# Retention ahead of the memory keys, the values inside the memory attention, and no lo parts on GpSimd

## The chip, the cores and the metric

The kernel runs on one core of a Trainium2 chip. The metric is the device time of one execution in microseconds. TensorE multiplies, ScalarE and VectorE do the element-wise work, GpSimd does a little of it, SyncE issues the loads. Weights stream from HBM into SBUF while the work goes on.

## The reference

Two blocks on 256 tokens of width 1024, in float32. The first block, cut to what matters here:

```python
x = x + parallel_mixer(rms_norm(x, norm_mix_w), w_in, ..., ret_gn_w, w_out)
x = x + memory_cross_attention(rms_norm(x, norm_mem_w), rms_norm(mem, norm_memkv_w),
                               w_mq, w_mkv, mem_q_norm_w, mem_k_norm_w, w_mo)
x = x + hierarchical_moe(rms_norm(x, norm_moe_w), w_group, w_router, ...)   # 32 experts, top 2
...
# parallel mixer: dilated attention beside retention in both directions
return jnp.concatenate([attn, ret], axis=-1) @ w_out
...
# memory attention
q = rms_norm(split_heads(h @ w_mq, MEM_HEADS, MEM_HEAD_DIM), q_norm_w) * (MEM_HEAD_DIM ** -0.5)
mk, mv = jnp.split(mem_h @ w_mkv, 2, axis=-1)
k = rms_norm(split_heads(mk, MEM_HEADS, MEM_HEAD_DIM), k_norm_w)
v = split_heads(mv, MEM_HEADS, MEM_HEAD_DIM)
```

The memory keys and values depend on `mem` alone, so they may be computed anywhere ahead of the memory attention. The second block has two layers, each a gated feed-forward, four token mixers, another feed-forward, with layer norms behind each.

## The kernel before

The 256 tokens are two token tiles of 128 partitions. Dense weights come in chunks of 1 MB (`raw`, a ring of four slots), in the order in which they are packed. To keep float32 accuracy each chunk, in two parts, is split exactly: `wh`, a rounded copy (ScalarE, L279), and `wl`, the rest (L283, a subtraction on VectorE or GpSimd). The tokens are split alike (`xh`, `xl`; ScalarE L391, VectorE L392). Every product is then three matmuls (`mm3`, L310 to L312). `s.pool_mod` and `s.on_pool` say which subtractions go to GpSimd: every fourth part, and some named ones.

Block 1 runs so: `mixer1` loads x, norms it with the gain `norm_mix_w` (a load that puts the 4 KB row on all 128 partitions), transposes it (L401) and projects; then dilated attention, the projections of retention, `mem_kv` (norm of the memory tokens, keys, values), `retention` and the out projection. `retention` has for each token tile two groups of heads: scores, a decay mask (`dtmp`, `dec`, `rsc`), value products (L718), then a norm per head (`normed`: statistics L679, L680, scaling L685, a power on GpSimd L418, scaling on ScalarE L690 and VectorE L692), and transposes of the result `rn`. `memory` norms, projects the queries (`mqn`, `mq`), then scores against the keys `mk`, softmax, values, out projection.

Meanwhile 21 chunks of the experts' weights are loaded into slots that come free (`moe_early`, `moe_slots`); the other 171 follow as the experts' products release slots. Ahead of the experts, `moe_start` computes the routes, and a branch (L889) goes into a long body only if an expert has more tokens than slots, which is not the case with these inputs.

All engines' instructions are put in order by a scheduler that simulates the program; the code's order decides which work exists at a time, and which slots of SBUF and PSUM it waits for. Transposes, retention's sums and the memory tokens' transposes share two PSUM banks (tag `tr`).

Of the kernel before, what the change touches and what calls it, by code (L numbers as in the profile page):

```python
# [26 lines left out]
# slots that the dense pools leave free, and those that memory()'s do  # L27
M_EARLY, M_MID = 6, 5

# projections (capitals; H: the heads of B) and attentions of the four mixers in the order of their issue  # L30
MIXERS = "BCHaDdAmw"
OUT = [k for k in MIXERS if k in "adwm"]
# the first gate and up tiles with tokens on partitions; the last down pairs with token tile 0 first, the norm of
# that tile after PLACE of the other's products
NAT, TAIL, PLACE = 2, 3, 4
# products of zeros that bring the tensor engine to its full clock while the first loads arrive
WARM = 18

# ------------------------------------------------------------------ host layout

def _nat(w):
    """[K, N] -> chunks [128, 4 k-tiles, <=512 columns], column groups outermost."""
    k, n = w.shape
    out = []
    for c in range(0, n, 512):
        g = w[:, c:c + 512].reshape(k // 128, 128, -1).transpose(1, 0, 2)
        for i in range(0, k // 128, 4):
            out.append(g[:, i:i + 4])
    return out


def _sq(w, halves=(0, 1)):
    """[1024, 1024] -> chunks [128, 4 k-tiles, 512 columns], halves of k outermost."""
# [4 lines left out]
def _trans(w):  # L58
    """[1024, N] -> chunks [128, 2 column tiles, 8 k-tiles, 128 columns]."""
# [19 lines left out]
def _pack_dense(i):  # L79
# [9 lines left out]
    ch += _nat(np.asarray(i["w_mkv"])[0])  # L89
    ch += _sq(np.asarray(i["w_out"])[0])  # L90
    ch += _nat(np.asarray(i["w_mq"])[0])
    ch += _sq(np.asarray(i["w_mo"])[0])
# [22 lines left out]
def _ffn_order():  # L115
    """Gate/up tiles and down pairs in the order of their use."""
# [55 lines left out]
def _pack_moe(i):  # L172
    """Per group of 4 experts: gate and up [k-tile][128, 4, 512], down [half][ff tile][128, 4, 512]."""
# [23 lines left out]
# ------------------------------------------------------------------ program  # L197

class Net:
    def __init__(s, ctx, tc, a, out):  # L200
        s.tc, s.nc, s.a, s.out = tc, tc.nc, a, out
        s.pos = 0
        s.on_pool = [None, None]
        s.pows, s.ahead = [], []
        s.dense_tags = ["a", "b"]
        s.nw, s.pool_mod = 0, 4
# [11 lines left out]
    # ---- storage  # L218
# [3 lines left out]
    def turn(s, tags):  # L222
        """The tags of a list in turn."""
# [3 lines left out]
    def banks(s):  # L227
        """Four accumulators, [token tile][half]."""
# [5 lines left out]
    def bcast(s, pool, name, n, off=0, tag=None, bufs=None, after=None):  # L234
        """A DRAM vector on every partition."""
# [7 lines left out]
    def column(s, pool, name, n, off=0, rep=1):  # L243
        """A DRAM vector down the partitions, rep times."""
# [7 lines left out]
    # ---- weights  # L252
# [12 lines left out]
    def weight(s, width=CH, parts=2, pool=None, own=None, cuts=1):  # L265
        """The next chunk, in parts, each as exact hi + lo, in the ring's tiles, pool's or own."""
# [3 lines left out]
        for i in range(parts):  # L270
# [13 lines left out]
            if eng is s.nc.gpsimd:  # L284
                s.pool_lo = i
# [5 lines left out]
    def own(s, p, i):  # L291
        """Tiles of pool p for a chunk."""
        return [[p.tile([128, CH // 2], F32R, name="own", tag=f"own{j}{k}{i}") for k in range(2)] for j in range(2)]

    def issue_after(s, i, j):
        """i, of the same engine as j, is issued after j."""
# [3 lines left out]
    def plan(s, spec):  # L300
        """Which of the next weight parts get their lo on GpSimd (not d), and after which of the last two powers."""
# [5 lines left out]
    # ---- products  # L307
# [6 lines left out]
    def dense_nat(s, x, n, done, stagger=False):  # L314
        """x @ W for n <= 512 columns, tokens on partitions; done(t, psum). stagger: token tile 0 first."""
# [25 lines left out]
    def dense_sq(s, x, done, halves=(0, 1), own=None, ahead=None):  # L341
        """x @ W for a square W, the k-tiles in halves, token tile 0 finished first; done(t, column half, psum).
        own: tiles for the parts of the last chunk."""
# [25 lines left out]
    def dense_trans(s, x, n, done):  # L369
        """(x @ W)^T for n <= 2 column tiles; done(i, psum[128, 256])."""  # L370
# [10 lines left out]
    # ---- operands  # L381
# [5 lines left out]
    def split(s, h, l, src, scale=None):  # L387
        """h + l = src * scale, exactly; scale a number or a column."""
# [8 lines left out]
    def transpose4(s, src, n=4, tag="tr"):  # L397
        """n blocks of 128 columns, transposed, in one bank."""
# [5 lines left out]
    def tsplit(s, x, t, src, k0=0, n=8, tag="tr"):  # L404
        """Token tile t of natural src (n k-tiles) into x[:, k0:]."""
# [7 lines left out]
    def rsqrt(s, v, n, scale, eps):  # L413
        """(v * scale + eps) ** -0.5; eps a number or a column."""
# [761 lines left out]
    def ln_state(s, p, x, li):  # L1176
# [3 lines left out]
        for t in range(NT):  # L1180
            xa.append(p.tile([128, D], F32, name=f"xa{t}"))
            i = s.nc.gpsimd.tensor_scalar(xa[t], x[t], ALPHA, None, op0=OP.mult)
            if li == 0:
                s.issue_after(i, s.pool_lo)
# [416 lines left out]
```

## Time and profile before

| | |
|---|---|
| time, median of 3 runs | 1754.07 us (1753.56 to 1755.35) |
| profiled execution, its span | 1753.4 us |
| TensorE busy | 1579.9 us, 90% |
| VectorE, ScalarE, GpSimd busy | 839.4, 657.0, 286.9 us |
| chain that ended last | TensorE 55%, loads 23%, VectorE 3% |
| TensorE's first expert gather | 284.73 us |

The profile gives no other time of the profiled execution than its span. The chain that ended last is followed back from the last instruction to whatever released it. Idle time of an engine counts only where that engine is waited for.

### The profile page before, as it was taken

Reading aid. Unit: us, or ns where it says so; the run is one execution under the profiler, and the core shown is the slowest. Engines: PE = TensorE matmul, PEld = TensorE weight load, DVE = VectorE, ACT = ScalarE, POOL = GpSimd, SP = SyncE. Lnnn points to the kernel's source line nnn. Section 1 sums busy time; section 2 is a strip of 40 time slices with the busy share of each in tenths; the row PEclk is TensorE's granted clock in tenths of the full one; section 3 lists DMA queues with packets and bytes.
Section 4 is the critical chain, followed back from the end, with each engine's and each line's share of the span. In section 5 each row is a group of like instructions: output and inputs, shape, how many; then the busy total and the mean of one; then the engine's idle time right before and its main releaser. Section 6 shows DMA issues by size and latency. Waiting matters only on the chain.

```text
span 1753.4 us, 24984 instructions
## 1 busy us (share of the span) xinstructions
PE 1579.9 (90%) x10070; PEld 1216.1 (69%) x10070; DVE 839.4 (48%) x1471; ACT 657.0 (37%) x1124; POOL 286.9 (16%) x253
## 2 busy tenths in 40 slices
PE   8999897877667767899999989999999999989998
PEld 6777784322211211599998769999999988779997
DVE  5657653100000000454477675556655667765555
ACT  4655441100000000344435745445444536734442
POOL 4223321100000000222224250000100032340000
PEclk9999998987878877999999989999999999989999
DMA  7444858999999999955554234556355634155552
GB/s 273 142 177 157 327 213 327 419 421 420 421 420 419 421 421 420 368 183 181 190 188 144 97 145 168 192 187 246 143 181 183 240 127 135 49 189 183 181 191 73
DMA packets 66186, 419.06 MB, mean 239 GB/s; under 512 B 10640, under 2 KB 12176, under 8 KB 18704
## 3 DMA queue, kind: packets, MB, share of 16 engines
q1 hardware_dynamic: 66064, 417.39, 62.8%
q8 instruction: 82, 1.34, 0.3%
q14 instruction: 40, 0.33, 0.1%
HBM read 416.32 MB, written 1.05 MB: 238 GB/s over the span
## 4 chain that ended last, share of the span: by engine, by line
PE 55%; DMA 23%; DVE 3%; POOL 1%; issue 1%; ACT 1%; DVEq 0%; SPq 0%; ACTq 0%; POOLq 0%
DMA mraw<-in_wm 23%; PE ps L310 17%; PE ps L312 17%; PE ps L311 17%; PE ps L401 1%; PE ps L480 1%; PE ps L950 1%; DVE xa L1169 1%; PE ps L970 0%; POOL rq L418 0%; PE ps L927 0%; DVE xl L392 0%; DVE lnst L1197 0%; DVE wl L283 0%; POOL ropet L1381 0%
## 5 line engine op out<-in xcount | busy, mean ns | idle before, releaser
L283 DVE TENSOR_TENSOR wl<-raw,wh 128x1024 fp32r<-128x1024 f32 (+2 forms) x314 | 389.3, 1250 | 302.0 <-ACT wh L279 301.1
L279 ACT ACTIVATE wh<-raw 128x1024 fp32r<-128x1024 f32 (+2 forms) x356 | 371.0, 1052 | 351.5 <-PE ps L311 181.1
L310 PE MATMUL ps<-xh,wh 128*128 128x256 f32 x1424 | 402.1, 282 | 3.4 <-ACT cv L1469 3.4
L312 PE MATMUL ps<-xh,wl 128*128 128x256 f32 x1424 | 401.4, 282 | 0.0
L311 PE MATMUL ps<-xl,wh 128*128 128x256 f32 x1424 | 401.0, 282 | 0.0
L310 PEld LDWEIGHTS ps<-xh,wh 128*128 128x128 f32 x1424 | 268.3, 188 | 6.6 <-ACT cv L1469 3.8
L311 PEld LDWEIGHTS ps<-xl,wh 128*128 128x128 f32 x1424 | 268.4, 189 | 1.4
L312 PEld LDWEIGHTS ps<-xh,wl 128*128 128x128 f32 x1424 | 268.4, 188 | 0.8
L950 PE MATMUL ps<-mraw,xg 128*32 128x512 f32 x1024 | 167.7, 758 | 77.4 <-DMA mraw<-in_wm 77.3
L312 PE MATMUL ps<-wh,xl 128*128 128x512 f32 (+3 forms) x520 | 190.1, 370 | 6.5 <-DVE xl L392 6.3
L310 PE MATMUL ps<-wh,xh 128*128 128x512 f32 (+3 forms) x520 | 190.5, 376 | 4.9 <-ACT xh L391 4.1
L311 PE MATMUL ps<-wl,xh 128*128 128x512 f32 (+3 forms) x520 | 191.9, 370 | 2.7 <-POOL wl L283 1.3
L950 PEld LDWEIGHTS ps<-mraw,xg 128*32 128x32 f32 x1024 | 25.6, 119 | 209.0 <-DMA mraw<-in_wm 173.0
L418 POOL TENSOR_TENSOR rq<-rv,mhalf 128x1 f32<-128x1 f32 (+4 forms) x46 | 46.9, 1020 | 728.1 <-DVE rv L416 720.4
L283 POOL TENSOR_TENSOR wl<-raw,wh 128x1024 fp32r<-128x1024 f32 x42 | 103.7, 2473 | 280.9 <-ACT wh L279 263.6
L956 DVE TENSOR_TENSOR mf<-ps,mf 128x512 f32<-128x512 f32 x8 | 5.5, 691 | 248.0 <-PE ps L950 244.1
L312 PEld LDWEIGHTS ps<-wh,xl 128*128 128x128 f32 x520 | 100.6, 194 | 23.2 <-DVE xl L392 10.4
L310 PEld LDWEIGHTS ps<-wh,xh 128*128 128x128 f32 x520 | 100.7, 195 | 22.7 <-ACT xh L391 7.6
L311 PEld LDWEIGHTS ps<-wl,xh 128*128 128x128 f32 x520 | 101.4, 195 | 18.4 <-POOL wl L283 3.4
L311 PE MATMUL ps<-wl,hf 128*128 128x512 f32 x256 | 100.1, 391 | 0.0
L312 PE MATMUL ps<-wh,hf 128*128 128x512 f32 x256 | 100.1, 391 | 0.0
L310 PE MATMUL ps<-wh,hf 128*128 128x512 f32 x256 | 98.2, 390 | 0.0
(357 smaller groups left out, 1981.0 us busy)
## 6 DMA issues: line engine op xcount, KB each, us to landing
mraw<-in_wm SPq DMA_DIRECT2D x191, 1024.0 KB, 19.9
raw<-in_wd SPq DMA_DIRECT2D x179, 1024.0 KB, 4.8
raw<-in_wd SPq DMA_DIRECT2D x8, 512.0 KB, 8.4
raw<-in_wd SPq DMA_DIRECT2D x4, 832.0 KB, 4.7
bc_ln_g<-in_ln_g SPq DMA_DIRECT2D x6, 512.0 KB, 5.7
bc_ln_b<-in_ln_b SPq DMA_DIRECT2D x6, 512.0 KB, 6.5
raw<-in_wd SPq DMA_DIRECT2D x4, 768.0 KB, 4.3
bias<-in_bias SPq DMA_DIRECT2D x4, 512.0 KB, 5.9
```

What stands on the lines that cost most here:

```text
L279: s.nc.scalar.activation(h[:, :n], rc, AF.Copy)
L283: i = eng.tensor_tensor(l[:, :n], rc, h[:, :n].bitcast(F32), op=OP.subtract)
L310: mm(out, lhsT=lh, rhs=rh, start=start, stop=False)
L311: mm(out, lhsT=lh, rhs=rl, start=False, stop=False)
L312: mm(out, lhsT=ll, rhs=rh, start=False, stop=stop)
L401: s.nc.tensor.transpose(ps[:, b * 128:b * 128 + 128], src[:, b * 128:b * 128 + 128], s.ident)
L418: s.last_pow = s.nc.gpsimd.tensor_tensor(q, r, s.mhalf[:, :n], op=OP.pow)
L480: s.nc.tensor.matmul(out, lhsT=v(j), rhs=pt[:, 2 * i + j], start=first and j == 0, stop=last and j == 1)
L950: nc.tensor.matmul(ps[32 * e:32 * e + 32], lhsT=xg[:, k, 32 * e:32 * e + 32], rhs=w[:, e * FF:e * FF + FF], start=k == 0, stop=k == NK - 1 ...
L956: nc.vector.tensor_tensor(f, gu[1], f, op=OP.mult)
L1169: nc.vector.scalar_tensor_tensor(z[:, cs], z[:, cs], mv[:, 0:1], g[:, cs], op0=OP.subtract, op1=OP.mult)
```

## The change

1. Order in block 1. `mem_kv` becomes `mem_k` (norm of the memory tokens and keys), called after `retention`, and `mem_v` (values), called in `memory` between the query projection and the scores. The weights are packed in the new order of use. The pools of the memory tokens lie on the other side of SBUF, and the out projection's extra tile has a pool of its own.
2. Start. The gain comes as a 4 KB row; a product with a column of ones puts it on all partitions, and VectorE copies it out of PSUM. The first raw chunk, in two halves, is issued ahead of token tile 1 of x. `moe_consts` (router weights and a triangle matrix) runs first.
3. No lo parts on GpSimd: `pool_mod` is 0 and no part is named, so 21 of block 1 and some 15 of the first feed-forward go to VectorE; eight in a later stage stay. One ordering rule that named the last such part is dropped.
4. The branch gets `preferred_fallthrough_block=False`: the short false path, a jump, stands behind the comparison, the body behind it.

Comments and docstrings go too, so line numbers differ.

```diff
-    ch += _nat(np.asarray(i["w_mkv"])[0])
+    mkv = np.asarray(i["w_mkv"])[0]
+    ch += _nat(mkv[:, :D])
     ch += _sq(np.asarray(i["w_out"])[0])
     ch += _nat(np.asarray(i["w_mq"])[0])
+    ch += _nat(mkv[:, D:])
...
-        s.on_pool = [None, None]
+        s.on_pool = []
...
-        s.nw, s.pool_mod = 0, 4
+        s.nw, s.pool_mod = 0, 0
...
-    def residual_out(s, x, o, ahead=None):
-        """x += o @ W for a square W; the operands before o are done with."""
-        w = s.xsp.tile([128, NK, S], F32R, name="xw", tag="xh").rearrange("p k n -> p (k n)")
+    def residual_out(s, x, o, ahead=None, pool=None):
+
+        w = (pool or s.xsp).tile([128, NK, S], F32R, name="xw", tag="xh").rearrange("p k n -> p (k n)")
...
     def mixer1(s):
+        s.moe_consts()
         x = [s.xp.tile([128, D], F32, name="x", tag=f"x{t}") for t in range(NT)]
...
+            one = p.tile([1, 128], F32, name="one")
+            s.nc.vector.memset(one, 1.0)
+            row = p.tile([1, D], F32, name="row")
+            s.nc.sync.dma_start(row, s.a["norm_mix_w"])
             for c in range(2):
                 cs = slice(c * 512, c * 512 + 512)
                 s.nc.sync.dma_start(x[0][:, cs], s.a["x"][:128, cs])
             s.nc.sync.dma_start(s.ident, s.a["ident"])
+            s.ahead = [s.raw(cuts=2)]
             s.nc.sync.dma_start(x[1], s.a["x"][128:])
-            wn = s.bcast(p, "norm_mix_w", D)
-            s.ahead = [s.raw(cuts=2)]
+            wn = p.tile([128, D], F32, name="wn")
+            for c in range(2):
+                cs = slice(c * 512, c * 512 + 512)
+                ps = s.bank("b")
+                s.nc.tensor.matmul(ps, lhsT=one, rhs=row[:, cs], start=True, stop=True)
+                s.nc.vector.tensor_copy(wn[:, cs], ps)
...
-            s.mem_kv()
-            s.on_pool = [None, False] * 3
             s.retention(r, o)
-        s.residual_out(x, o)
+            s.mem_k()
+        with ExitStack() as ctx:
+            s.residual_out(x, o, pool=s.pool(ctx, "xw1", side="right"))
         return x
...
-        ms = s.rms_operand(load, "norm_memkv_w")
+        s.ms = s.rms_operand(load, "norm_memkv_w", side="right")
         with ExitStack() as ctx:
-            p = s.pool(ctx, "memk")
+            p = s.pool(ctx, "memk", side="right")
             for c in range(2):
-                s.dense_nat(ms, 512, lambda t, ps: s.mem_normed(p, s.mk, c, t, ps, None))
+                s.dense_nat(s.ms, 512, lambda t, ps: s.mem_normed(p, s.mk, c, t, ps, None))
+
+    def mem_v(s):
+
         for c in range(2):
             def done(t, ps):
                 cs = slice(c * 512, c * 512 + 512)
-                nc.scalar.activation(s.mv[:, t, cs], ps, AF.Copy)
-            s.dense_nat(ms, 512, done)
+                s.nc.scalar.activation(s.mv[:, t, cs], ps, AF.Copy)
+            s.dense_nat(s.ms, 512, done)
...
-        s.moe_consts()
-        o = s.xsplit()
...
             s.moe_early(c0)
+            s.mem_v()
+            o = s.xsplit()
+            s.moe_slots(s.xsp, ["xl"])
...
-        with s.tc.If(cnt > CAP):
+        with s.tc.If(cnt > CAP, preferred_fallthrough_block=False):
             s.overflow(ht, x, r, hT, acc, late)
```

The first place is the start on VectorE. Before, the gain tile `bc_norm_mix_w` is a load, and the scales of x (`rms`) come first; `xl` is the lo part of the transposed tokens, `wl` a lo part of a weight chunk.

```order
L986 TENSOR_SCALAR ssb_156<-ss_155 128x1
L416 TENSOR_SCALAR rv_160<-ss_155,ssb_156 128x1
L508 SCALAR_TENSOR_TENSOR rms_128<-x_91,rq_136,bc_norm_mix_w_123 128x512 x2
L508 SCALAR_TENSOR_TENSOR rms_154<-x_92,rq_162,bc_norm_mix_w_123 128x512 x2
L392 TENSOR_TENSOR xl_94<-ps_139,xh_93 128x4x128
L392 TENSOR_TENSOR xl_94<-ps_147,xh_93 128x4x128
L392 TENSOR_TENSOR xl_94<-ps_165,xh_93 128x4x128
L283 TENSOR_TENSOR wl_267<-raw_264,wh_266 128x1024
L392 TENSOR_TENSOR xl_94<-ps_173,xh_93 128x4x128
L283 TENSOR_TENSOR wl_355<-raw_352,wh_354 128x1024
```

After, `wn` is the gain copied out of PSUM, `rv` and `ssb` belong to the norm of x.

```order
L285 TENSOR_TENSOR wl_269<-raw_141,wh_268 128x1024
L285 TENSOR_TENSOR wl_273<-raw_141,wh_272 128x1024
L548 COPY wn_145<-ps_146 128x512
L999 TENSOR_SCALAR ssb_180<-ss_179 128x1
L548 COPY wn_145<-ps_149 128x512
L508 SCALAR_TENSOR_TENSOR rms_152<-x_106,rq_160,wn_145 128x512
L416 TENSOR_SCALAR rv_184<-ss_179,ssb_180 128x1
L508 SCALAR_TENSOR_TENSOR rms_152<-x_106,rq_160,wn_145 128x512
L508 SCALAR_TENSOR_TENSOR rms_178<-x_107,rq_186,wn_145 128x512 x2
L285 TENSOR_TENSOR wl_291<-raw_288,wh_290 128x1024
L392 TENSOR_TENSOR xl_109<-ps_163,xh_108 128x4x128
```

The copies of the gain, and with them the scales, have moved behind two lo parts of the first weight chunk.

The second place is TensorE at the end of retention. Before: `rv,rsc` are the value products, `ident,rn` the transposes of the normed output, `wl,xh` and the like dense products (here of the out projection). The piece shows the first transposes of token tile 1.

```order
L310 MATMUL ps<-wh,xh 128x512
L311 MATMUL ps<-wl,xh 128x512
L312 MATMUL ps<-wh,xl 128x512
L310 MATMUL ps<-wh,xh 128x512
L401 MATMUL ps<-ident,rn 128x128
L311 MATMUL ps<-wl,xh 128x512
L312 MATMUL ps<-wh,xl 128x512
L310 MATMUL ps<-wh,xh 128x512
L311 MATMUL ps<-wl,xh 128x512
L312 MATMUL ps<-wh,xl 128x512
L310 MATMUL ps<-xw,xh 128x512
```

After, from the last scores (`rqp,rk`) on: the first two transposes are of token tile 0, the four at the end of both tiles.

```order
L311 MATMUL ps<-rqp_211,rk_212 128x256
L312 MATMUL ps<-rqp_210,rk_213 128x256
L401 MATMUL ps<-ident,rn 128x128 x2
L728 MATMUL ps<-rv_214,rsc 128x128
L728 MATMUL ps<-rv_215,rsc 128x128
L728 MATMUL ps<-rv_214,rsc 128x128
L728 MATMUL ps<-rv_215,rsc 128x128
L728 MATMUL ps<-rv_214,rsc 128x128
L728 MATMUL ps<-rv_215,rsc 128x128
L728 MATMUL ps<-rv_214,rsc 128x128
L728 MATMUL ps<-rv_215,rsc 128x128
L401 MATMUL ps<-ident,rn 128x128 x4
```

The dense products that stood around the transposes are gone from here: `mem_k` now comes after `retention`, and its first products stand behind the transposes.

The third place is TensorE in the memory attention. Before, `ident,mqn` are the transposes of the normed queries, and `mk,mq` the scores.

```order
L401 MATMUL ps<-ident,mqn 128x128 x8
L310 MATMUL ps<-mk_82,mq_1858 128x256
L311 MATMUL ps<-mk_90,mq_1858 128x256
L310 MATMUL ps<-mk_82,mq_1858 128x256
L311 MATMUL ps<-mk_90,mq_1858 128x256
L312 MATMUL ps<-mk_82,mq_1859 128x256
L310 MATMUL ps<-mk_82,mq_1858 128x256
L311 MATMUL ps<-mk_90,mq_1858 128x256
L312 MATMUL ps<-mk_82,mq_1859 128x256
```

After, the products of the memory values (`wh,xh` and the like) are there too.

```order
L310 MATMUL ps<-wh,xh 128x512 x2
L310 MATMUL ps<-mk_82,mq_1725 128x256
L311 MATMUL ps<-mk_90,mq_1725 128x256
L310 MATMUL ps<-mk_82,mq_1725 128x256
L311 MATMUL ps<-mk_90,mq_1725 128x256
L311 MATMUL ps<-wl,xh 128x512
L312 MATMUL ps<-wh,xl 128x512
L310 MATMUL ps<-wh,xh 128x512
L311 MATMUL ps<-wl,xh 128x512
L312 MATMUL ps<-wh,xl 128x512
L401 MATMUL ps<-ident,mqn 128x128 x4
L311 MATMUL ps<-wl,xh 128x512
```

The value products now stand between the first scores and the transposes of the queries.

## Rows read from the trace of the kernel before

**Rows 1.** page, the 40 slices; busy tenths of TensorE and of the DMA engines

```profile
PE   8999897877667767899999989999999999989998
...
DMA  7444858999999999955554234556355634155552
```

**Rows 2.** timeline, start of the experts' stage: VectorE, SyncE, TensorE (start us, us, instructions)

```profile
281.81 0.61 DVE L918 SCALAR_TENSOR_TENSOR G<-slots,sg,ge 128x128 f32<-128x128 f32 x2
...
284.60 0.33 SPq L824 DMA_DIRECT2D mraw<-in_wm  x1
...
284.73 1.19 PE L927 MATMUL ps<-G,xg 128*128 128x128 f32 x4 [5.49 <-PEq L889]
```

**Rows 3.** timeline of VectorE, ScalarE, TensorE and SyncE, first 20 us

```profile
10.53 2.74 DVE L508 SCALAR_TENSOR_TENSOR rms<-x,rq,bc_norm_mix_w 128x512 f32<-128x512 f32 x4 [0.60 <-DMA bc_norm_mix_w<-in_norm_mix_w]
...
11.34 1.32 PE L401 MATMUL ps<-ident,rms 128*128 128x128 f32 x8 [3.17 <-DVE rms L508]
...
11.70 1.06 ACT L279 ACTIVATE wh<-raw 128x1024 fp32r<-128x1024 f32 x1 [2.01 <-DMA raw<-in_wd]
...
16.14 0.63 PE L312 MATMUL ps<-wh,xl 128*128 128x512 f32 x1
...
16.37 3.85 SPq L801 DMA_DIRECT2D tri<-in_tri  x1
```

**Rows 4.** timeline, norm chain of retention's token tile 1, VectorE and ScalarE

```profile
182.58 0.89 DVE L679 BATCH_NORM_STATS2 b<-ps 128x6 f32<-128x128 f32 x4 [0.97 <-PE ps L718]
...
186.54 0.68 ACT L690 ACTIVATE rn<-rn,rq 128x128 f32<-128x128 f32 x2
...
186.67 1.23 DVE L283 TENSOR_TENSOR wl<-raw,wh 128x1024 fp32r<-128x1024 f32 x1 [1.25 <-ACT wh L279]
```

**Rows 5.** groups by line and shape, GpSimd, 0 to 284 us

```profile
L283 POOL TENSOR_TENSOR wl<-raw,wh 128x1024 fp32r<-128x1024 f32 x19 | 46.0, 2426 | 63.5 <-ACT wh L279 46.2 <-issue 17.3
```

**Rows 6.** waits of TensorE, 0 to 340 us (total, times, longest)

```profile
PE ps L311 <- POOL wl L283: 1.3, 2, 0.9
```

**Rows 7.** timeline of GpSimd and VectorE during a subtraction on GpSimd

```profile
167.80 2.58 POOL L283 TENSOR_TENSOR xw<-raw,xw 128x1024 fp32r<-128x1024 f32 x1
...
168.04 2.49 DVE L708 TENSOR_SCALAR dtmp<-dist,lg 128x256 f32<-128x256 f32 x1
...
171.05 0.34 DVE L708 TENSOR_SCALAR dtmp<-dist,lg 128x256 f32<-128x256 f32 x1
```

**Rows 8.** timeline of TensorE in retention

```profile
161.91 1.13 PE L718 MATMUL ps<-rv,rsc 128*128 128x128 f32 x8 [1.25 <-DVE rsc L713]
...
166.92 0.36 PE L310 MATMUL ps<-rqp,rk 128*128 128x256 f32 x1
...
167.72 0.40 PE L310 MATMUL ps<-wh,xh 128*128 128x512 f32 x1
...
176.26 0.33 PE L401 MATMUL ps<-ident,rn 128*128 128x128 f32 x1 [1.90 <-ACT rn L690]
...
178.22 0.47 PE L401 MATMUL ps<-ident,rn 128*128 128x128 f32 x1 [1.63 <-DVE rn L692]
```

**Rows 9.** table by stages: busy of the engines, granted clock, DMA share, GB/s

```profile
176.00:180.00 4.00, 2.11 (x10) 1.92 (x11) 4.00 (x2) 1.45 (x3) 4.00 (x2) 0.62 0.19 37
...
180.00:184.00 4.00, 4.00 (x17) 3.67 (x17) 3.03 (x8) 0.60 (x1) 0.40 (x1) 0.53 0.85 301
...
228.00:232.00 4.00, 3.78 (x19) 3.79 (x20) 2.86 (x8) 0.39 (x1) 0.70 (x1) 0.57 0.30 127
```

**Rows 10.** groups by line and shape, ScalarE, squares of the memory tokens

```profile
L984 ACT ACTIVATE rms<-memx 128x512 f32<-128x512 f32 x4 | 2.5, 622 | 0.0
```

**Rows 11.** timeline of TensorE in the memory attention

```profile
226.54 0.39 PE L310 MATMUL ps<-mk,mq 128*128 128x256 f32 x1 [1.29 <-ACT mq L391]
...
228.22 0.58 PE L312 MATMUL ps<-mk,mq 128*128 128x256 f32 x1 [0.68 <-DVE mq L392]
```

**Rows 12.** the branch's line, TensorE's weight queue

```profile
L889 PEldq COMPARE_BRANCH  x1: 3903/3903/3903, 280.5 to 280.5; - x1
```

More of the change, by code (lines that the diff above doesn't have):

```diff
@@ L283, in weight @@
             i = eng.tensor_tensor(l[:, :n], rc, h[:, :n].bitcast(F32), op=OP.subtract)
-            if eng is s.nc.gpsimd:
-                s.pool_lo = i
             if after:
@@ L509, in rms, with rms_operand @@
             yield c, z
-    def rms_operand(s, src, name):
+    def rms_operand(s, src, name, side=None):
         hs = s.xsplit()
         with ExitStack() as ctx:
-            p = s.pool(ctx, "rms")
+            p = s.pool(ctx, "rms", side=side)
             wn = s.bcast(p, name, D)
@@ L720, in retention, with mem_k @@
                 normed(t, y)
-    def mem_kv(s):
+    def mem_k(s):
         nc = s.nc
@@ L845, in moe_early @@
         s.moe_slots(s.pool(ctx, "mring0", side="right"), [f"m{i}" for i in range(M_EARLY)])
-        s.moe_slots(s.xsp, ["xl"])
     def moe_start(s, ctx, c3, x):
@@ L1181, in ln_state @@
             xa.append(p.tile([128, D], F32, name=f"xa{t}"))
-            i = s.nc.gpsimd.tensor_scalar(xa[t], x[t], ALPHA, None, op0=OP.mult)
-            if li == 0:
-                s.issue_after(i, s.pool_lo)
+            s.nc.gpsimd.tensor_scalar(xa[t], x[t], ALPHA, None, op0=OP.mult)
         st = [s.st.tile([128, 2 + 2 * t, 6], F32, name="lnst", tag=f"lnst{t}", bufs=2) for t in range(NT)]
```

## The prediction

> **What bounds the kernel now.** I read four views, in this order. First the page's 40 slices. From the eighth to the seventeenth (307 to 745 us) the DMA engines show 9 tenths and TensorE 6 to 8 [rows 1]: the experts' stage waits for weights, not for engines; later it is TensorE that shows 9. Then the timeline where that stage starts. Its loads go ahead only as slots come free: SyncE issues the next load at 284.60, as TensorE begins the first gather at 284.73 [rows 2]. So a shift of the end of block 1 moves the stream of loads, and with it the end of the run, one to one. All that the change touches lies ahead of 284.7 us, except some 15 subtractions in the first feed-forward layer. Third, the timeline of TensorE in block 1 with what it waited for: nearly everything there is products, so what counts is TensorE's idle time, and the time in which it works at a lower granted clock. Fourth, the order of instructions of both kernels, for what stands between the end of one chain of small operations and the product that needs it.
>
> Durations come from the profiled execution, whose span is 1753.4 us. The median of the runs shown is 1754.07; the 0.7 between I take as what lies around the span, unchanged.
>
> **The start (term A).** Before, the gain row is loaded on all partitions (512 KB). The first scale on VectorE starts at 10.53, released by that load; the first transposes follow at 11.34. The first half of the first weight chunk is there at 11.70, and products that need both parts of the tokens run from 16.14 [rows 3]. After, the broadcast load is gone, so the load queue carries about 148 + 64 KB of router data, x tile 0, ident and then the raw chunk. By 10.53 the old queue had moved x, ident and the gain, 1.57 MB; by 11.70 2.10 MB; 2.2 us per MB. The second raw half now ends at 1.78 MB, so lands near 11.0. The order of VectorE puts both lo subtractions of that chunk ahead of the copies of the gain out of PSUM. That gives: 11.0, plus a split on ScalarE 1.06, a lo 1.23 [rows 4], two copies and the first scale at 0.69 each (2.74 / 4 by the four scales; that a copy of the same size takes as long is an estimate): transposes at 15.4 instead of 11.3, 4.1 late. From there four scales and one more lo, 4 x 0.69 + 1.23, and one operation more of that size for xl, 0.69, counted from the copies' end at 14.7, put the first product with xl at 19.4 instead of 16.14, 3.2 late. I take +3.5. Bounds: 0, if the raw halves come with x and the copies are done by 10.5. Above, the router load is now the first on SyncE's queue and has 148-byte rows; the load behind it (tri) took 3.85 us to issue [rows 3], and x now stands behind both. All of it on top gives +8. I leave this out of the middle value since at 16 us other loads were on the queue ahead of it (the first chunk had only come in at 11.70), and at the start there are none.
>
> **No GpSimd subtractions (term B).** 19 of them take 2.43 us each [rows 5], two more fill the xw tiles. On VectorE one takes 1.23 [rows 4]: 21 x 1.23 = 26 us more work in 285 us. What comes back: TensorE waited 1.3 us for GpSimd's parts [rows 6], and VectorE is freed of a neighbour. While GpSimd's subtraction ran from 167.80 to 170.38, the small scaling that takes 0.34 at 171.05 took 2.49 at 168.04 [rows 7]. I take -1, the wait gone less a little queueing on VectorE. Bounds -3 (wait gone and freed chains) to +3 (two or three chains standing behind a lo each). The 15 subtractions in the first feed-forward lie beside products, in the stage where TensorE shows 9 tenths [rows 1]: 0. Without that cover they would cost up to 15 x 1.23 = 18.
>
> **Retention and memory keys (term C).** Before, the product of memory keys and values is spread through retention. TensorE idles 1.25, 1.90 and 1.63 us there [rows 8], 4.8 together. Its clock is granted at 0.62 in 176 to 180 with 2.11 us of work and 0.53 in 180 to 184 with 4.00 [rows 9] (1 is 2.4 GHz, so 0.53 is nearly all at 1.2): 2.11 x 0.38 + 4.00 x 0.47 = 2.7 lost. Together 7.5. After, memory keys come later; they need the PSUM banks that the transposes of retention still hold. TensorE's order then has, between the last value product of token tile 0 and the transposes of its normed output, six score products only; between tile 1's and its transposes, none. The chain between them is shown by tile 1 before: statistics from 182.58, the last scaling on ScalarE ends 186.54 + 0.68 = 187.22 [rows 4], so 4.6 us, which the out projection's products covered. Tile 0: 4.6 less six products (167.72 - 166.92 = 0.8 [rows 8]) plus one masking operation and two small waits that VectorE's order puts into that chain, 1.5 (an estimate; 0.7 of it is an operation of the size of a scale): 5.3. Tile 1: 4.6 less 0.3 for two extra operations that the chain before held: 4.3. A third hole: on ScalarE the split of a gate chunk now stands behind squares of the memory tokens, four at 0.62 [rows 10], of which I count 2.4 as exposed. Sum 12.0 idle. After such holes the clock was granted at about half for the next 6 us of work; one lasting longer costs about 4 by the same measure (6 us at 0.6 and 1.5 times as much work). 16 against 7.5: I take +8, rounded down since the third hole is the least sure. Bounds: -2, if the chains run undisturbed (0.3 to 1 us shorter each), the third hole is nothing, and the clock stays up; +12, if also the transposes of the memory tokens, which wait for the same banks, open a hole of 2 to 4.
>
> **Memory values between query and scores (term D).** Before, TensorE waits 1.29 and 0.68 us for the split queries [rows 11] and then has 3.78 us of work at 0.57 of the clock in 228 to 232 [rows 9], a loss of 1.6: 3.6 in all. After, the 96 products of the values stand around these places. I take -3.6; bounds -4.3 (a later wait of 0.7 for the probabilities goes too) and 0 (the new products come with lo subtractions of their own on VectorE, which is where the split queries wait).
>
> **The branch (term E).** On TensorE's weight queue the branch takes 3.9 us [rows 12], and TensorE waits 5.49 us until 284.73 [rows 2]. The one-hots that it needs next are there at 281.81 + 0.61 = 282.4 [rows 2], so at most 2.3 us could be had. With the changed layout the false path is a short block directly behind the comparison, but that block holds only a jump over the same body. I take 0; bounds -2.2 to +0.1. The Trainium skill, "Runtime: NRT & Kernel Launch", section "Instruction fetch mechanics", says that prefetch is purely sequential and that a taken branch to a place outside the fetched window forces a fetch before work goes on. The 3903 ns agree with a fetch. By that rule the jump that is left costs the same; by a layout that needs no fetch the sum would be 2.2 lower (R4).
>
> **Sum.** +3.5 - 1 + 8 - 3.6 + 0 = +6.9. 1753.4 + 6.9 + 0.7 = 1761.0 us. Its own range is 1757.5 to 1766, by halving the distance to the bounds of A and C.
>
> **The rivals.**
> R1, the other side: GpSimd's subtractions were the brake on VectorE. Place: the norm chains of retention and the attention chains ahead of them. A small scaling took 2.49 instead of 0.34 there [rows 7]. If VectorE is freed, B is -3, the retention holes shrink to the lower bound, C = -2.2, and D is as forecast: 3.5 - 3 - 2.2 - 3.6 = -5.3, 1748.8 us. It decides if the wait in front of each of the two groups of transposes stays under about 2.3 us and the clock does not fall. Against it: the chain of tile 1 took its 4.6 us with no subtraction running on GpSimd [rows 4]. The Trainium skill, "SBUF — State Buffer", section "Who interferes with whom", has the two engines share a port pair under an exclusive lock. The 2.49 beside 0.34 agrees; by that rule all of VectorE's excess beside GpSimd would go. Chance 0.20.
> R2: the holes open as forecast, but the clock stays at full and half of the late start is caught up, since the first chunks were ahead of need: A +1.5, B -1, C +4.5, D -3.6: +1.4, 1755.5 us. For it: that a fall follows a wait is seen at two places only [rows 9]. Against it: both followed waits shorter than the ones expected. Chance 0.21.
> R3: the router load in front delays x, since the next load issues 3.85 later. A becomes +7.4: 1764.9, with a slow retention (C +12) 1769 us. Against it: the queue is empty then. Chance 0.13.
> R4: the layout does free TensorE of the long jump: 1761.0 - 2.2 = 1758.8 us. Against it: the unconditional jump is still taken. Chance 0.05.
> The forecast has 0.41.
>
> **How the numbers follow.** A change under 0.2%, 3.5 us, cannot be told from none here; the borders are 1750.6 and 1757.6. Faster is nearly all of R1: 0.18 and 0.02 of the others, 0.20. Same is R2 with a little of R1 and of the forecast: 0.25. Slower is the rest, 0.55. The range must reach toward R1 and R3: 1749.5 to 1767 leaves out about half of R1 and the far end of R3, 0.2 together.
>
> **What would show it.** A: first transposes at about 15 us, with both gain copies behind two lo subtractions; at 11 or less the term is wrong, at 19 R3 holds. B: no wait for lo beyond 0.5 us, small scalings at 0.35 everywhere. C: two waits of 4 to 5 us in front of the transposes of the normed output, with a granted clock near 0.5 behind them; waits under 2.3 and full clock are R1. D: no wait in front of the first products of keys with queries, and full clock there. E: the branch at about 3.9 us on the weight queue again. The forecast as a whole is wrong if the first gather of the experts begins before 285 us; by the sum it begins near 291.6.

## The result and the profile after

| | before | after |
|---|---|---|
| time, median of 4 runs each, taken in turns | 1753.82 us (1752.44 to 1755.35) | 1770.74 us (1769.76 to 1772.56) |
| span of the profiled execution | 1753.4 us | 1769.3 us |
| TensorE's first expert gather | 284.73 us | 299.35 us |
| from there to the first transposes of block 2 | 428.70 us | 430.08 us |
| the rest of the span | 1039.97 us | 1039.87 us |

The ratio is 1.0094 (1.0080 to 1.0109). Slower was the likeliest sign, but 1761.0 was forecast and the time lies 3.7 us above the range. Of 15.9 us in the span 14.6 arose ahead of the gather, where the prediction had put all of it, and 1.4 between the gather and block 2; block 2 gave nothing. One execution further down took 1984.15 us at a mean granted clock of 0.743; it counts nowhere, and its kernel ran again.

The waits of TensorE up to 345 us, after (us in total, times, longest):

```profile
PE ps L401 <- ACT rn L700: 9.5, 2, 5.7
...
PE ps L310 <- ACT pr L451: 2.4, 1, 2.4
PE ps L401 <- DVE mqn L760: 2.2, 1, 2.2
PE ps L310 <- ACT wh L281: 2.1, 2, 1.9
...
PE ps L312 <- DVE xl L392: 1.6, 1, 1.6
```

The wait for GpSimd's parts [rows 6] is gone. Two waits in front of `rn` and one for `wh` are the holes of term C. Three were not in the sum: for `pr` (the probabilities of the memory attention), for `mqn` (here the normed keys of the memory tokens) and for `xl` (the tokens' lo parts at the norm of `memory`).

The start on VectorE and on ScalarE, after (start, duration, instructions):

```profile
10.43 1.22 DVE L285 TENSOR_TENSOR wl<-raw,wh 128x1024 fp32r<-128x1024 f32 x1 [3.38 <-ACT wh L281]
12.46 1.22 DVE L285 TENSOR_TENSOR wl<-raw,wh 128x1024 fp32r<-128x1024 f32 x1 [0.81 <-ACT wh L281]
13.60 0.68 DVE L548 COPY wn<-ps 128x512 f32<-128x512 f32 x1
...
14.86 0.74 DVE L508 SCALAR_TENSOR_TENSOR rms<-x,rq,wn 128x512 f32<-128x512 f32 x1
```

```profile
12.80 0.63 ACT L997 ACTIVATE rms<-x 128x512 f32<-128x512 f32 x1 [0.37 <-DMA x<-in_x]
```

The order of [rows 3] has turned as forecast: two lo parts, copies, then the scale at 14.86 instead of 10.53. Token tile 1 of x is now squared only at 12.80, since its load stands behind the raw chunk.

TensorE in retention, after:

```profile
126.24 0.69 PE L401 MATMUL ps<-ident,rn 128*128 128x128 f32 x2 [5.67 <-ACT rn L700]
126.72 3.62 PE L728 MATMUL ps<-rv,rsc 128*128 128x128 f32 x16
...
134.56 0.44 PE L401 MATMUL ps<-ident,rn 128*128 128x128 f32 x2 [3.79 <-ACT rn L700]
```

Its granted clock there and at three later places (window, us; busy of PE, PEld, DVE, ACT, POOL; PEclk; DMA share, GB/s):

```profile
124.00:128.00 4.00, 1.76 (x8) 1.76 (x9) 1.39 (x7) 0.69 (x2) 1.01 (x1) 0.58 0.22 91
128.00:132.00 4.00, 2.77 (x13) 2.36 (x12) 1.62 (x9) 0.60 (x1) 0.00 (x0) 0.56 0.00 0
...
168.00:172.00 4.00, 3.97 (x13) 3.20 (x14) 2.00 (x5) 2.05 (x3) 0.70 (x1) 0.63 0.00 0
...
192.00:196.00 4.00, 3.71 (x10) 2.95 (x11) 2.37 (x5) 0.33 (x2) 0.56 (x1) 0.61 1.02 426
...
248.00:252.00 4.00, 3.68 (x20) 3.44 (x18) 2.11 (x7) 1.79 (x6) 0.00 (x0) 0.63 0.00 0
```

Where [rows 9] had one fall in retention, there is one again. Behind the waits for `mqn`, `xl` and `pr` the clock is lower too: 0.61 to 0.63 as the mean of four us, between the two levels of 1.2 and 2.4 GHz. What each costs is the busy time by the missing share: 3.97 x 0.37 = 1.5 us at 168, 3.71 x 0.39 = 1.4 at 192, 3.68 x 0.37 = 1.4 at 248.

Where the 14.6 us came from: I compared the time at which TensorE has done the same number of dense products, so each term holds idle time and clock together. From retention to the memory attention the kernel after still has the 96 products of the values to do; there they are counted as done, at 0.2275 us each, their distance at full clock (21.8 us, an estimate). Start (A) +3.2; lo parts between start and retention (B) -0.2; retention and keys (C) up to the end of the out projection +9.4; the norm of `memory` behind it +2.7; the memory attention (D) -0.6; the branch (E) +0.1. Behind the gather another +1.4. Sum 16.0, against 15.9 of the span.

### The profile page after: what moved, and what is told of

Its sections match the earlier page's. It is cut to its first block, busy times and chain, and to the rows that moved or that the text cites. A ratio compares the mean times of both kernels' runs of the same rounds, so it can differ in the third digit from the quotient of the medians.

```text
span 1769.3 us, 24966 instructions
## 1 busy us (share of the span) xinstructions
PE 1583.5 (89%) x10074; PEld 1219.9 (69%) x10074; DVE 847.6 (48%) x1511; ACT 657.2 (37%) x1124; POOL 198.1 (11%) x216
## 3 DMA queue, kind: packets, MB, share of 16 engines
HBM read 415.80 MB, written 1.05 MB: 236 GB/s over the span
## 4 chain that ended last, share of the span: by engine, by line
PE 54%; DMA 23%; DVE 3%; POOL 1%; issue 1%; ACT 1%; DVEq 0%; SPq 0%; ACTq 0%; POOLq 0%
DMA mraw<-in_wm 23%; PE ps L310 17%; PE ps L312 17%; PE ps L311 17%; PE ps L401 1%; PE ps L480 1%; PE ps L963 1%; DVE xa L1182 1%; POOL rq L418 0%; DVE lnst L1208 0%; PE ps L940 0%; POOL ropet L1392 0%; DVE xa L1207 0%; DVE xl L392 0%; PE ps L1451 0%
## 5 line engine op out<-in xcount | busy, mean ns | idle before, releaser
L285 DVE TENSOR_TENSOR wl<-raw,wh 128x1024 fp32r<-128x1024 f32 x348 | 420.6, 1219 | 311.4 <-ACT wh L281 310.4
L983 PE MATMUL ps<-mraw,fT 128*32 128x512 f32 x512 | 75.2, 690 | 19.2 <-DMA mraw<-in_wm 16.4
```

The costliest lines, as they stand in the source:

```text
L285: i = eng.tensor_tensor(l[:, :n], rc, h[:, :n].bitcast(F32), op=OP.subtract)
L983: nc.tensor.matmul(ps[32 * e:32 * e + 32], lhsT=fT[:, b, 32 * e:32 * e + 32], rhs=w[:, e * 512:e * 512 + 512], start=b == 0, stop=b == 3, ...
```

## The experiments

In the expectations T1 is the theory that the new order of block 1 opens holes in retention and costs most; the other numbers are its rivals, said in words there. Ratios are to the kernel before; "gather" is the start of TensorE's first expert gather (299.35 after). Each gather is read from one execution.

A gather adds up stages that an edit does not touch. So the table gives, against after, how much earlier (-) or later (+) TensorE does the same work, by stages. "Start" is up to the 61st dense product, "retention" from there to the end of the out projection, "norm" the norm of `memory` up to the transposes of its second token tile, "attention" from there to the transposes of the updated x, "routes" from there to the gather.

| us against after | start | retention | norm | attention | routes | gather |
|---|---|---|---|---|---|---|
| old order of block 1 (values at 0.2275 each) | +1.0 | -9.6 | -2.7 | +0.3 | -0.2 | -11.1 |
| keys early | -1.2 | -1.0 | -2.8 | -3.3 | -0.4 | -8.6 |
| other banks | +0.9 | -9.2 | -0.1 | -3.8 | +0.1 | -12.1 |
| old start | -4.0 | +0.1 | 0.0 | 0.0 | +0.1 | -3.8 |
| copies first | -0.1 | +2.4 | -1.6 | -3.8 | +0.2 | -2.9 |
| lo parts on GpSimd | +2.6 | +5.8 | -1.6 | -2.9 | +0.4 | +4.3 |
| old branch | +0.5 | +0.2 | 0.0 | 0.0 | 0.0 | +0.7 |
| small exponential | +0.6 | +0.4 | 0.0 | -2.8 | +0.3 | -1.6 |
| lo parts of the tokens first | -0.3 | +0.1 | -2.4 | -3.2 | -0.1 | -5.8 |

Two things limit what may be read from it. The six kernels whose edit leaves the start alone and keeps the lo parts differ there by -1.2 to +1.0, so a difference of one us at the gather shows nothing. And an edit reaches further than its own stage, through the order that the scheduler makes: the attention is 2.9 to 3.8 shorter in four kernels whose edit lies elsewhere.

**The old order of block 1** (with the packing and pools that belong to it), everything else as after.

```diff
+            s.mem_k()
+            s.mem_v()
             s.retention(r, o)
-            s.mem_k()
...
-            s.mem_v()
```

> The changed kernel with part 1 alone taken back: memory keys and values ahead of retention as before, start, lo parts and branch as changed. Theory T1 (read from the two traces: the order of block 1 leaves the norm chains of retention uncovered, 9.4, and lets the clock fall at the memory norm, 2.7, for 0.6 gained at the scores): 1770.7 - 11.5 = 1759.2 us, the two waits of 5.7 and 3.8 us in front of the transposes of rn gone. Rival T2 (the lo parts moved to VectorE make the chains late, the order only shows it): it stays above 1766, with a wait of 3 us or more still at rn.

1756.02 us, ratio 1.0012 (1.0003 to 1.0021), gather 288.20: 11.15 earlier, 9.6 of it in retention and 2.7 at the norm, less a start that came 1.0 later. So the order carries most. 4.0 more came from block 2 (rest of the span 1035.86 instead of 1039.87), where nothing was edited. At the first norm behind a mixer there TensorE waits 3.7 us for `x` in both; what follows, after and then in this kernel:

```profile
1052.00:1056.00 4.00, 1.69 (x8) 1.56 (x8) 3.58 (x9) 0.56 (x1) 1.89 (x2) 0.63 0.31 82
1056.00:1060.00 4.00, 3.74 (x16) 3.13 (x14) 3.94 (x3) 0.63 (x2) 4.00 (x3) 0.51 1.01 418
1060.00:1064.00 4.00, 1.41 (x9) 1.41 (x10) 4.00 (x4) 0.00 (x0) 4.00 (x2) 0.91 0.44 125
```

```profile
1041.00:1045.00 4.00, 1.71 (x10) 1.29 (x10) 3.93 (x10) 1.04 (x2) 1.89 (x2) 0.93 0.36 92
1045.00:1049.00 4.00, 3.11 (x14) 2.68 (x13) 4.00 (x4) 0.15 (x1) 4.00 (x3) 0.64 1.00 414
1049.00:1053.00 4.00, 3.39 (x27) 3.19 (x27) 3.88 (x3) 0.50 (x1) 4.00 (x2) 1.00 0.32 68
```

The same wait is followed by a low clock for about twice as long in the first. By busy time and missing share that is 2.6 us against 1.2, so some 1.4 of the 4.0 (an estimate); where the rest arose is open. Over all traces the stretch from block 2 on takes 1035.8 to 1042.4 us. So an edit in block 1 is judged by the trace up to the gather, not by the total.

**Only the keys ahead of retention; the values stay late.**

```diff
+            s.mem_k()
             s.retention(r, o)
-            s.mem_k()
```

> The changed kernel with the memory keys ahead of retention and the values still in the memory attention. T1 (the norm chains lack filler because the keys' products can't start): the two waits at rn shrink to under 2.5 each, third hole gone, the first gather at 288 to 291, 1759 to 1762 us; the memory norm's clock fall and the wait for the probabilities stay. Rival T6 (the values taken out of retention are the missing filler, the keys alone don't help): gather at 296 or later.

1763.88 us, ratio 1.0054 (1.0037 to 1.0071), gather 290.74: -8.6. One wait in front of `rn` is left, 2.4; the third hole is gone. But this does not show that the place of the keys carries the 11.15: by the table retention gives back 1.0 only, while new waits of 1.60 (`rms`), 1.51 (`wl`), 1.44 and 1.16 (`xh`) stand around the early keys. The norm gives 2.8, with a wait of 0.55 for `xl` instead of 1.56; 3.3 come from the attention and 1.2 from the scatter of the start.

**Other PSUM banks for the memory tokens' transposes** (tag `b` for `tr`).

```diff
-        s.ms = s.rms_operand(load, "norm_memkv_w", side="right")
+        s.ms = s.rms_operand(load, "norm_memkv_w", side="right", tag="b")
```

> The changed kernel with one word changed: the memory tokens' transposes use the PSUM banks of tag b instead of the two that retention's sums and transposes hold, so that the memory keys can start inside retention. T1 (the keys can't fill the norm chains because of the banks): the waits of 5.7 and 3.8 us at rn and the clock fall behind them gone, first gather 8 to 10 earlier than 299.4, 1760 to 1763 us. Rival T6 (only the values, moved out of retention, are missing): gather at 296 or later, 1767 or more.

1760.28 us, ratio 1.0034 (1.0020 to 1.0048), gather 287.27: -12.1, 9.2 of it in retention, without moving a line of the program. No wait for `rn` is left. TensorE in this kernel:

```profile
121.08 1.03 PE L401 MATMUL ps<-ident,rms 128*128 128x128 f32 x8
122.65 0.50 PE L310 MATMUL ps<-wh,xh 128*128 128x512 f32 x1 [0.54 <-ACT xh L391]
...
125.67 1.09 PE L401 MATMUL ps<-ident,rms 128*128 128x128 f32 x4 [2.29 <-DVE xl L392]
...
133.75 0.60 PE L401 MATMUL ps<-ident,rn 128*128 128x128 f32 x4
```

The transposes of the memory tokens (`ident,rms`) come before those of `rn`, and key products fill the chain. That shows the step of the prediction that the keys come late because the banks are held. Another 3.8 belong to the memory attention, where the scheduler's order is another and the wait for `pr` is 0.2.

**The old start.**

```diff
     def mixer1(s):
-        s.moe_consts()
...
-            s.ahead = [s.raw(cuts=2)]
             s.nc.sync.dma_start(x[1], s.a["x"][128:])
-            wn = p.tile([128, D], F32, name="wn")
...
+            wn = s.bcast(p, "norm_mix_w", D)
+            s.ahead = [s.raw(cuts=2)]
```

> The changed kernel with the old start: the gain by a 512 KB load, router constants in the memory attention, x ahead of the weights. T1: 3.0 less, 1767.7 us, first transposes near 11.4 instead of 15.7. Rival T3 (a later start is caught up in the attention stage, where TensorE waits for other engines anyway): 1770.7, the first gather of the experts still at 299.4.

1766.73 us, ratio 1.0079 (1.0063 to 1.0095), gather 295.51: -3.8. First transposes at 11.40, and 4.0 earlier from the 61st product on. The late start is not caught up later.

**The new start, with the copies of the gain ahead of the lo part.**

```diff
+            if s.gain is not None:
+                s.issue_after(i, s.gain)    # i: the first lo part, gain: the copies
```

> The changed kernel with one issue order more: the first weight chunk's lo subtractions on VectorE only after the copies of the gain. T1 (the place of the copies behind two lo parts is what makes the start late): transposes at about 11 instead of 15.7, the products 1.5 to 3 earlier, 1768 to 1769 us. Rival T5 (the order of the loads makes the start late, x tile 1 being behind the weights and landing at 12.4): transposes of tile 0 early, but the run within 0.7 of 1770.7.

1769.18 us, ratio 1.0088 (1.0071 to 1.0105), gather 296.45, first transposes at 13.70. VectorE in this kernel:

```profile
8.69 0.69 DVE L552 COPY wn<-ps 128x512 f32<-128x512 f32 x1 [1.61 <-PE ps L551]
12.78 0.15 DVE L1003 TENSOR_SCALAR ssb<-ss 128x1 f32<-128x1 f32 x1 [3.40 <-ACT rms L1001]
12.89 0.75 DVE L512 SCALAR_TENSOR_TENSOR rms<-x,rq,wn 128x512 f32<-128x512 f32 x1
```

The copy is ready at 9.4, but a statistic of token tile 1 stands in front of the scale and waits for the late x. The transposes are 2.0 earlier, the 61st dense product is 0.1 earlier: the place of the copies alone gives nothing back, as T5 has it, and the -2.9 of the gather arise at the norm and in the attention, with +2.4 in retention against them. With the old start, which changes both, 4.0 come back; the raw chunk ahead of x is thus enough for the late start.

**The lo parts on GpSimd again.**

```diff
-        s.on_pool = []
+        s.on_pool = [None, None]
...
-        s.nw, s.pool_mod = 0, 0
+        s.nw, s.pool_mod = 0, 4
...
+            s.on_pool = [None, False] * 3
             s.retention(r, o)
```

> The changed kernel with lo parts on GpSimd again (every fourth, and the named ones at the start and in retention). T1: within 1 of the changed kernel, 1770 to 1772, since by the delays at equal work the waits that go (1.8) come back as others by 100 us. T2: 6 to 9 less, 1762 to 1765, the waits at rn under 3 us.

1777.27 us, ratio 1.0132 (1.0116 to 1.0147), gather 303.60: both theories wrong, it is 6.5 slower than after. TensorE waits 7.12 and 4.00 in front of `rn` and 3.4 for `qn`. GpSimd and VectorE in this kernel, ahead of the first of these:

```profile
116.89 4.81 POOL L285 TENSOR_TENSOR wl<-raw,wh 128x1024 fp32r<-128x1024 f32 x2 [3.06 <-ACT wh L281]
...
127.85 2.33 POOL L285 TENSOR_TENSOR wl<-raw,wh 128x1024 fp32r<-128x1024 f32 x1
```

```profile
117.16 2.30 DVE L721 TENSOR_SCALAR dtmp<-dist,lg 128x256 f32<-128x256 f32 x1 [0.42 <-ACT dec L724]
...
131.18 0.48 DVE L705 TENSOR_SCALAR rn<-rn,rq 128x128 f32<-128x128 f32 x2 [3.02 <-POOL rq L420]
```

The slow small scaling of [rows 7] is there again, 2.30. And a part of 2.33 on GpSimd stands ahead of the power that `rn` needs, and VectorE waits 3.02 for it. That is in retention, +5.8; another +2.6 arise at the start, and 2.7 between the gather and block 2.

**The kernel before, with nothing changed but the lo parts** (`pool_mod` 0, no part named).

> The kernel before with one change: no lo parts on GpSimd. If the gain of 6.5 belongs to the lo parts everywhere: 1747 to 1749. If it belongs to the new order, whose uncovered chains stand beside them (theory T11): 1752 to 1755, since the gathers of the two traces leave -0.4 for it once order and start are taken off.

1752.40 us, ratio 0.9990 (0.9981 to 0.9999), gather 281.63: 3.1 earlier than before, 2.8 of it between the start and the end of the out projection; the total shows about half.

**The old layout of the branch.**

> The changed kernel with the old layout of the branch. T1 (the jump over the body is fetched twice, and the first expert products stand with gaps of 0.6 and 0.8 us behind it): 1.4 less, 1769.3, eight first products in 1.9 us instead of 3.6. Rival T4 (the gaps come from the state of the loads or the clock and not from the layout): 1770.7, the gaps still there.

1770.52 us, ratio 1.0092 (1.0078 to 1.0105), gather 300.01: no difference that the scatter of the start would not explain. The branch's line on TensorE's weight queue, after (count, min/median/max ns, start; in this kernel there is one, of 4003 ns):

```profile
L902 PEldq COMPARE_BRANCH  x2: 95/2005/3915, 295.0 to 295.3; - x2
```

**A small exponential ahead of `mem_v`, so that ScalarE's table comes early.**

```diff
+            nc.scalar.activation(s.stat(2, "early"), s.rm, AF.Exp)
             s.moe_early(c0)
             s.mem_v()
```

> The changed kernel with one small exponential on ScalarE more, behind the query norms, so that the table for Exp is loaded before the scores. Theory T7 (the wait of 2.4 us for the probabilities that took the place of the removed ones is the table load of 1.28 us, needed since retention's gate now comes last on ScalarE): the wait falls to about 1.1, the run 1.3 to 2.7 earlier, 1768 to 1769.4. Rival T8 (the weight split of 1.05 us ahead of the exponential in ScalarE's queue makes the wait): wait above 2, 1770.7.

1767.56 us, ratio 1.0074 (1.0058 to 1.0091), gather 297.79: -1.6; in the attention, where the edit is, -2.8. ScalarE and TensorE after, then TensorE in this kernel:

```profile
242.69 1.05 ACT L281 ACTIVATE wh<-raw 128x1024 fp32r<-128x1024 f32 x1
243.76 1.28 ACT L451 ACT_TABLE_LOAD   x1
```

```profile
246.13 0.39 PE L310 MATMUL ps<-mk,mq 128*128 128x256 f32 x1 [2.42 <-ACT pr L451]
```

```profile
245.70 0.39 PE L310 MATMUL ps<-mk,mq 128*128 128x256 f32 x1 [0.99 <-ACT pr L451]
```

```profile
248.00:252.00 4.00, 3.31 (x23) 2.92 (x23) 2.79 (x10) 3.25 (x11) 0.00 (x0) 1.00 0.37 100
```

Without the load the wait falls from 2.42 to 0.99, and the last row, this kernel's clock, shows 1.00 where after had 0.63. The load alone is not the cause, though. With the copies first, ScalarE has it at the same place, behind a split and ahead of the first probabilities:

```profile
238.09 1.28 ACT L455 ACT_TABLE_LOAD   x1
```

```profile
238.09 0.39 PE L316 MATMUL ps<-wh,xl 128*128 128x512 f32 x1
...
246.48 0.38 PE L314 MATMUL ps<-mk,mq 128*128 128x256 f32 x1 [0.17 <-ACT pr L455]
```

There TensorE still has value products beside the load, and the wait for `pr` is 0.17. After, its last value product starts at 241.77, ahead of the load at 243.76. The load costs where the scheduler has used up the value products before it.

**The tokens' lo parts ahead of two weight lo parts at the norm of `memory`** (an ordering rule on VectorE), in two runs.

> The changed kernel with the lo parts of the tokens at the memory norm issued ahead of the second and third lo part of the query weights on VectorE. Theory T9 (the 1.56 us wait there lets the clock fall, 1.8): wait under 0.7, no fall at 192 to 196 us, 1768 to 1769. Rival T10 (the weights' lo parts are as late then): the wait moves to them, 1770.7 or more.

> The kernel of f_xl again, for a profile. T9: no wait over 0.7 for xl at the memory norm and a granted clock of 1.0 from 188 to 200 us; first gather at 296 to 297.5.

1764.95 us, ratio 1.0066 (1.0049 to 1.0082), and 1766.07, ratio 1.0069 (1.0051 to 1.0088); gather 293.51: -5.8. TensorE before and after, VectorE before and after, then the clock in this kernel:

```profile
200.61 0.51 PE L312 MATMUL ps<-wh,xl 128*128 128x512 f32 x1 [0.57 <-DVE xl L392]
```

```profile
192.29 0.50 PE L312 MATMUL ps<-wh,xl 128*128 128x512 f32 x1 [1.56 <-DVE xl L392]
```

```profile
196.94 2.35 DVE L283 TENSOR_TENSOR wl<-raw,wh 128x1024 fp32r<-128x1024 f32 x2
```

```profile
188.62 2.35 DVE L285 TENSOR_TENSOR wl<-raw,wh 128x1024 fp32r<-128x1024 f32 x2
190.89 0.68 DVE L498 TENSOR_TENSOR x<-ps,x 128x512 f32<-128x512 f32 x1
...
191.55 1.28 DVE L392 TENSOR_TENSOR xl<-ps,xh 128x512 fp32r<-128x512 f32 x2
```

```profile
192.00:196.00 4.00, 3.73 (x18) 2.35 (x17) 2.96 (x5) 0.22 (x1) 0.55 (x1) 1.00 1.01 424
```

At equal work 2.4 are won here, wait and clock. Another 3.2 come in the memory attention, where the scheduler's order is another now and ScalarE's table is loaded at 235.09 beside products.

**All repairs together**: after with the old start, the other banks, the early exponential and the ordering rule; once with the branch option and once without.

> A candidate: the changed kernel with the old start and the three edits of c_fill, d_exp and f_xl. T1, T7 and T9 together: first gather at 282 to 285 and 1750 to 1755 us. If the edits don't add: 1757 to 1762.

> The kernel of combo without the branch's option. If the layout delays the start of the experts' stage: 1.4 to 2.2 less, 1751 to 1751.6, and the first load behind the branch issued 0.1 us ahead of the gather. If not: 1753.0.

1753.04 us, ratio 0.9996 (0.9986 to 1.0006), gather 281.77; and 1752.72, ratio 0.9995 (0.9986 to 1.0004), gather 282.39. The whole loss is undone, and nothing is won over before.

**Two tries at a faster version**: the old order, and the early keys, each with the router data late and the copies of the gain first.

> A candidate: the changed kernel with block 1 in the old order, the router constants in the memory attention again, and the gain's copies ahead of the first lo parts. T1: 1756.0 less the start's 3 to 4, 1752 to 1753. T5: 1755 to 1756.

> The same candidate with the memory keys ahead of retention but the values in the memory attention. T1: as k_early less 3 to 4, 1756 to 1758; T6: 1763 or more.

1759.04 us, ratio 1.0024 (1.0014 to 1.0035), and 1766.17, ratio 1.0070 (1.0053 to 1.0087). Neither beats the kernel that it is built on (1756.02 and 1763.88); the first has runs from 1755.2 to 1760.1, so two orders of the start that differ little are not told apart by it.

## Why the prediction was right or wrong

**A, +3.5: right.** Transposes at 15.66 (15.4 forecast), 3.2 at equal work, 4.0 by the run with the old start, where kernels with the same start differ by up to 2. What the prediction did not have is that x tile 1, behind the raw chunk, holds the start as long as the lo parts do: with the copies first, nothing came back. R3 is out: the load `tri` was issued in 0.57 us, not 3.85.

**B, -1: -0.2 between before and after, but no fixed property of the edit.** Taking the lo parts off GpSimd is worth 3.1 us at the gather in the old order. In the new one it is worth 4.3 there and 6.5 of the total; retention alone is 5.8 longer with them, since a part in front of the small powers has no products to hide it. R1's mechanism thus exists, but the holes opened all the same. The Trainium skill, "SBUF — State Buffer", section "Who interferes with whom", has one of the two engines blocked while the other holds the port pair that they share. VectorE's 2.30 beside GpSimd's part agrees. The wait of 3.02 for the power is of the runs alone.

**C, +8: the mechanism right, the size a little off.** Forecast were holes of 5.3, 4.3 and 2.4; the rows show 5.67, 3.79 and 1.90, and 0.58 and 0.56 of the clock behind the first. The other banks, which take these holes away, give 9.2 back. C is 9.4 instead of 8: the wait of 2.2 for the normed keys with its lower clock (1.5) was not in the sum, and the clock behind the holes cost 3.2 (124 to 140 us, by busy time and missing share) where 4 was put. R2 is out, since the clock fell.

**D, -3.6: this is the step that failed.** "The 96 products of the values stand around these places": they do, and the waits of [rows 11] are gone. The step took it that these products cover the way to the probabilities too; their wait stood in a bound alone, at 0.7. Two things put a wait of 2.42 there, followed by four us at 0.63, so that -0.6 was left.

First, the gate of retention is another function of ScalarE's than the exponential. ScalarE's table loads, before, and then the one for the gate after:

```profile
110.21 1.28 ACT L632 ACT_TABLE_LOAD   x1
...
156.11 1.28 ACT L711 ACT_TABLE_LOAD   x1
```

```profile
118.13 1.28 ACT L642 ACT_TABLE_LOAD   x1
```

Before, the gate was computed from 111.52 on, the exponential's table was loaded again at 156.11 for the decays, and the probabilities found it there. After, the gate at 119.42 is the last of the two to be computed before them, so the load at 243.76 stands directly in front of the first probabilities, with a split of 1.05 ahead of it. Second, the scheduler had used up the value products by then. Take one of the two away and nearly the whole forecast is there: 2.8 come back with the early exponential, 2.9 to 3.8 in the kernels whose order leaves value products beside the load. The prediction asked which operations stand ahead of the waits that it knew, not which function ScalarE had computed last, nor where the value products end.

**A term that was missing: the norm of `memory`, +2.7.** Before, TensorE's wait for `xl` at this place was 0.57 at a clock of 1.00; after, 1.56 and 0.61. The lo parts taken from GpSimd are not the cause: on VectorE the same two lo parts stand ahead of the update of x and of `xl` in both kernels. Without lo parts on GpSimd the old order still has a wait of 0.58, and with them the new one has 1.56. It goes with the place of the keys: 0.5 to 0.6 in all six kernels that have them ahead of retention, 1.6 in all seven that have them behind and lack the ordering rule. Before, VectorE began this row of operations at 195.20, 2.76 ahead of the transposes; after, at 186.89, 1.61 ahead of them. With the ordering rule the wait is gone and 2.4 come back. The prediction had no term here, nor a price for the clock behind a short wait. The clock's part is not certain, however: with the copies first, the wait is there again, the clock stays up, and the norm costs 1.6 less:

```profile
194.57 0.50 PE L316 MATMUL ps<-wh,xl 128*128 128x512 f32 x1 [1.55 <-DVE xl L396]
```

```profile
194.00:198.00 4.00, 3.43 (x15) 2.85 (x16) 2.65 (x5) 0.62 (x2) 0.56 (x1) 1.00 1.01 426
```

What decides between the two is open.

**E, 0: right; R4 is out.** The option left a comparison and a jump of 3915 ns where one of 3903 stood [rows 12]. The rule of the Trainium skill that the prediction cited ("Runtime: NRT & Kernel Launch", section "Instruction fetch mechanics"), that a taken branch to a place that is not fetched yet waits for a fetch, agrees.

**Behind the gather, +1.4, forecast 0: open.** The first expert products with weights take 1.94 us before and 3.60 after:

```profile
286.63 1.94 PE L950 MATMUL ps<-mraw,xg 128*32 128x512 f32 x8
```

```profile
301.24 3.60 PE L963 MATMUL ps<-mraw,xg 128*32 128x512 f32 x8
```

The repaired kernel needs 430.95 to block 2 with the branch option and 428.41 without, which speaks for the layout; but after without it needs 430.87, which speaks against it. Over all traces, the twelve kernels with the option need 429.5 to 432.8, and of the four without it three need 428.4 to 428.7. It was not settled.

The forecast's 6.9 and the 15.9 of the span thus differ by D (3.0), the norm (2.7), C (1.4), the place behind the gather (1.4) and B (0.8), less A (0.3): 9.0. The 0.7 that the prediction put around the span is the difference of two executions; in the runs above, time and span of one and the same differ by 1.7 to 2.0.

## What to carry to other kernels

Work that is moved away from a chain of small operations takes its cover with it: look which banks the moved work needs before counting on it to fill the gap. Price a wait on TensorE with the clock that may fall behind it, as a range: here waits of 1.56 and 2.42 us cost 3.0 and 3.8 with the clock behind them, while one of 1.55 was followed by full clock. When ScalarE's work changes its order, list its functions in that order, look for a table load in front of whoever is waited for, and see whether TensorE has products left beside it. Judge an edit stage by stage: through the scheduler's order a kernel's edit changed stages further down by up to 3.8 us.

## What had not been expected of the hardware

The same 3.7 us wait in block 2 was followed by about eight us at 0.51 to 0.63 in one kernel and by four at 0.64 in another, with the same lines ahead of it; with no edit nearby the rest of the span moved by 4.0 us. A wait of 1.56 at the norm of `memory` was followed by 0.61, one of 1.55 by 1.00. The issue of the load `tri` took 3.85 us with other loads on the queue [rows 3], and 0.57 at the queue's start, after; what the longer one waited for is not shown.

```profile
1.36 0.57 SPq L815 DMA_DIRECT2D tri<-in_tri  x1
```
